# One core, two transformer blocks in float32: the recurrent mixer's steps laid out anew

## The chip, the cores and the metric

One core of a Trainium2 chip runs the whole kernel in one launch. The metric is device time in microseconds (us): 3861.58 us before the change, the median of three runs (3859.82 to 3863.74).

## What is computed

The reference runs two blocks one after the other on 512 tokens of width 1024, all in float32. The change touches one part of the second block, its recurrent mixer, which takes the normalised activations `h` and returns a term that is added to the residual:

```
proj = h @ w_in                       # 1024 -> 2 x 1024: gate, rec
rec  = causal_depthwise_conv(rec)     # 4 taps over the tokens, + bias
r, i = sigmoid(blockwise(rec, w_a) + b_a), sigmoid(blockwise(rec, w_x) + b_x)   # 8 blocks of 128x128
log_a = -8 * r * softplus(-lam);  a = exp(log_a)
bx = sqrt(-expm1(2 * log_a)) * (i * rec)
h_t = a_t * h_(t-1) + bx_t            # scan over the tokens
out = (gelu(gate) * h) @ w_out
```

## The kernel before

Activations lie transposed, features on 128 partitions and the 512 tokens along the free axis, so a width of 1024 is eight chunks ("heads" below, m = 0 to 7). Every float32 product is made of three matmuls on pieces of reduced precision: weights and activations are each split into a high and a low half, and high x high, high x low and low x high are added up in PSUM. A product of one 128-column block of weights with all eight chunks is 24 matmuls (`fm`, lines 317 to 321), one with the output weights by chunk (`wout_k`, lines 767 to 769) 12.

**Weights.** The class `Stream` (from line 51) takes all weight blocks of the kernel in one planned order. A block is fetched by the sync queue into one of three slots (line 102), ScalarE writes its high half `wh` (line 132), VectorE its low half `wl` (line 135), each into one of four buffers. `get` hands out the next block, and before that issues the halves of the blocks up to two places ahead. The engines work through their queues in the order in which the program issues instructions; there is no scheduler that reorders them.

**The mixer** is `rec`, lines 782 to 899. It has sixteen steps u. Steps 0 to 7 make the eight chunks of the recurrent branch, steps 8 to 15 those of the gate branch; each is one product `q` of 24 matmuls. In a step, in the order of issue:
- In steps 2 to 9 `gates_mm(u - 2)` takes two blocks of weights, `ra` and `rx`, and multiplies the halves of chunk u - 2 with both (6 matmuls).
- The chunk that the step before convolved is split into halves (`split`, lines 302 and 303).
- The step's own product is taken up. In steps 0 to 7 VectorE scales it by the row norm `rB` (`conv_start`, line 811), ScalarE makes the last tap and the bias (line 812), GpSimd the first tap (line 818), VectorE the two others (line 820), and GpSimd adds the first one in (line 822). In steps 8 to 14 VectorE scales it into `G` (`evac_g`, line 839).
- `gates(u - 2)`: two sigmoids on ScalarE (lines 803, 805), one product on GpSimd (line 806).
- `decays`: exp and tanh on ScalarE (lines 826, 827) for two heads at a time, in steps 4, 6, 8 and 9; ahead of them `advance` issues the halves of further weights.
- `newton`: one Newton step on the reciprocal that stands behind `a`: a copy on ScalarE (line 832), two operations on VectorE (833, 834), two on GpSimd (835, 836).
- In step 11 the eight square roots (line 884); `scan` for heads 0 to 3 in steps 12 to 14: Gelu on ScalarE (842), a product on GpSimd (843), three operations on VectorE, one of them the scan over the tokens (844 to 846).

After the loop the eight results are split into `hl` (new tiles), with the scans of heads 4 to 7 between them. Then `wout_k` multiplies chunk by chunk, two chunks to a block of weights, and `wout_end` makes the last four output chunks. A block's halves are issued two places ahead, so those of the third output block are issued by `wout_k` for chunk 0, behind everything of the loop.

The row norm `rB` comes from `stat1` (eight small matmuls, line 348; a power on GpSimd, line 354; VectorE, line 360) and `stat2` (a broadcast on TensorE, line 366, copied by ScalarE, line 367), both called after step 0's product.

PSUM has eight banks: two pairs `D`, one pair `E` and two single banks `M`. `dbl` gives pairs of D and E in turn; products and gate pairs of the mixer each take a pair.

Of the kernel before, what the change touches and what calls it, by code (L numbers as in the profile page):

```python
# [15 lines left out]
ALU = mybir.AluOpType  # L16
# [30 lines left out]
def colblock(w, c0, n=P):  # L47
    return w[:, c0:c0 + n].rearrange("(k p) n -> p k n", p=P)

# [132 lines left out]
class Kernel:  # L182
# [553 lines left out]
    def plan_rec(self):  # L736
# [4 lines left out]
        def blk(m):  # L741
            ws.add(("ra", m), wa[m].unsqueeze(1))
            ws.add(("rx", m), wx[m].unsqueeze(1))
# [38 lines left out]
    def rec(self, d, on_x):  # L782
# [10 lines left out]
        taps = {}  # L793

        def gates_mm(m):
            w = (self.ws.get(("ra", m)), self.ws.get(("rx", m), 1))
            q = self.dbl()
            for i in range(2):
                self.fm([(q[:, i], sl)], w[i], xhl[m % 3], nk=1)
            return q  # L800

        def gates(m, q):
# [3 lines left out]
            nc.gpsimd.tensor_tensor(X[:, m], X[:, m], g, ALU.mult)  # L806

        def conv_start(m, q):
            taps[m] = c = self.tmp(TT, tag="ca", bufs=3)[:, :T + 3]
            nc.gpsimd.memset(c[:, 0:3], 0.0)  # L810
            nc.vector.tensor_tensor(c[:, 3:], q, d.rB, ALU.mult)
            nc.scalar.activation(X[:, m], c[:, 3:], AF.Identity, bias=self.v("rec_conv_b_2", m),
                                 scale=self.v("rec_conv_w_2", 24 + m))

        def conv_end(m):
            c, x = taps.pop(m), X[:, m]
            t = self.tmp(T, tag="sq")
            nc.gpsimd.tensor_scalar(t, c[:, 0:T], self.v("rec_conv_w_2", m), 1.0, ALU.mult, ALU.mult)
            for j in (1, 2):
                nc.vector.scalar_tensor_tensor(x, c[:, j:j + T], self.v("rec_conv_w_2", 8 * j + m), x, ALU.mult,  # L820
                                               ALU.add)
            nc.gpsimd.tensor_tensor(x, x, t, ALU.add)
# [6 lines left out]
        def newton(m):  # L829

            z, a, e, f = R[:, m], A[:, m], self.tmp(T, tag="ta"), self.tmp(T, tag="sq")
            nc.scalar.activation(f, a, AF.Copy, scale=0.5, bias=0.5)
            nc.vector.scalar_tensor_tensor(e, z, 1.0, a, ALU.add, ALU.mult)
            nc.vector.scalar_tensor_tensor(e, e, 1.0, z, ALU.subtract, ALU.add)
            nc.gpsimd.tensor_tensor(e, e, f, ALU.mult)
            nc.gpsimd.tensor_tensor(a, a, e, ALU.subtract)
# [3 lines left out]

        def scan(m):
            nc.scalar.activation(G[:, m], G[:, m], AF.Gelu_apprx_tanh)
            nc.gpsimd.tensor_tensor(X[:, m], X[:, m], R[:, m], ALU.mult)
# [4 lines left out]
        ahead = {4: range(2), 6: range(2, 4), 8:range(4,6), 9: range(6, 8)}  # L848
        after = {4: (0,), 5: (1,), 6: (2,),7:(3,),8:(4,),9:(5,), 10: (6, 7)}
        scans = {12: (0,1), 13: (2,), 14: (3,)}  # L850


        for u in range(2 * NK):
            m = u % NK
            w = self.ws.get(("rr" if u < NK else "rg", m))
            q = self.dbl()[:, 0]
            self.fm([(q, sl)], w, d.x)
            if u == 0:
                self.stat1(d)
                self.stat2(d)  # L860
            g = gates_mm(u - 2) if 2 <= u < NK + 2 else None
            if 1 <= u < NK + 1:
                h, l = xhl[(u - 1) % 3]
                self.split(h[:, 0], l[:, 0], X[:, u - 1])
            if u < NK:
                conv_start(m, q)
                conv_end(m)
            else:
                for i in scans.get(u, ()):
                    scan(i)  # L870
                if m < NK - 1:
                    evac_g(m, q)
            if g is not None:
                gates(u - 2, g)

            if u in ahead:
                self.ws.advance(self.ws.i, 0)
            for i in ahead.get(u, ()):
                decays(i)
            for i in after.get(u, ()):  # L880
                newton(i)
            if u == NK + 3:
                for i in range(NK):
                    nc.scalar.activation(R[:, i], R[:, i], AF.Sqrt)
# [1869 lines left out]
```

## Time and profile before

| | |
|---|---|
| device time, median of three runs | 3861.58 us |
| device time of the profiled execution | 3859.96 us |
| its span, first to last instruction | 3858.2 us |
| TensorE, matmuls busy | 3656.6 us (95% of the span) |
| VectorE busy | 2621.0 us (68%) |
| ScalarE busy | 1577.4 us (41%) |
| GpSimd busy | 720.7 us (19%) |

Times in the trace count from the first instruction. PE is TensorE, DVE is VectorE, ACT is ScalarE, POOL is GpSimd. A busy share says how much of the time an engine had an instruction in work; matmuls overlap, so their durations add up to more than the time between their starts. What stands in square brackets at the end of an instruction's row is how long its engine idled before it, and whose instruction ended that.

### The profile page before, as it was taken

Reading aid. Unit: us, or ns where it says so; the run is one execution under the profiler, and the core shown is the slowest. Engines: PE = TensorE matmul, PEld = TensorE weight load, DVE = VectorE, ACT = ScalarE, POOL = GpSimd, SP = SyncE. Lnnn points to the kernel's source line nnn. Section 1 sums busy time; section 2 is a strip of 40 time slices with the busy share of each in tenths; the row PEclk is TensorE's granted clock in tenths of the full one; section 3 lists DMA queues with packets and bytes.
Section 4 is the critical chain, followed back from the end, with each engine's and each line's share of the span. In section 5 each row is a group of like instructions: output and inputs, shape, how many; then the busy total and the mean of one; then the engine's idle time right before and its main releaser. Section 6 shows DMA issues by size and latency. Waiting matters only on the chain. (4 is left out here: it accounts for less than half of the span.)

```text
span 3858.2 us, 54617 instructions
## 1 busy us (share of the span) xinstructions
PE 3656.6 (95%) x21148; PEld 3150.7 (82%) x21148; DVE 2621.0 (68%) x4287; ACT 1577.4 (41%) x2606; POOL 720.7 (19%) x755
## 2 busy tenths in 40 slices
PE   7898999999999978999999998999999999889999
PEld 5887978888887777877789886788977998678898
DVE  7887877765646286544477777677765777766776
ACT  2354523222225275422344447444443444464443
POOL 6334231000012074100100016100020000460000
PEclk8999999999999999999999999999999999899999
DMA  5300043433422442233333322333334333213332
GB/s 176 107 1 23 1 148 95 125 112 118 137 68 88 139 134 77 82 90 90 90 98 102 96 78 81 97 87 96 95 114 124 98 99 99 83 42 102 98 103 75
DMA packets 570400, 363.48 MB, mean 94 GB/s; under 512 B 17719, under 2 KB 546605, under 8 KB 570141
## 3 DMA queue, kind: packets, MB, share of 16 engines
q1 hardware_dynamic: 564317, 346.21, 30.7%
q0 software_dynamic: 3520, 9.59, 0.8%
q8 instruction: 167, 2.74, 0.3%
q10 hardware_dynamic: 2304, 4.20, 0.3%
q14 instruction: 92, 0.75, 0.1%
HBM read 345.72 MB, written 14.20 MB: 93 GB/s over the span
## 5 line engine op out<-in xcount | busy, mean ns | idle before, releaser
L135 DVE TENSOR_TENSOR wl<-ws,wh 128x1024 fp32r<-128x1024 f32 (+3 forms) x474 | 583.3, 1240 | 313.6 <-ACT wh L132 311.2
L132 ACT ACTIVATE wh<-ws 128x1024 fp32r<-128x1024 f32 (+3 forms) x474 | 457.6, 978 | 588.5 <-DVE ws L454 257.3
L562 PE MATMUL D<-ah,wl 128*128 128x256 f32 x1344 | 380.2, 283 | 11.1 <-DVE wl L135 11.1
L560 PE MATMUL D<-ah,wh 128*128 128x256 f32 x1344 | 377.1, 281 | 1.6 <-DVE gu L602 1.6
L561 PE MATMUL D<-al,wh 128*128 128x256 f32 x1344 | 376.4, 280 | 0.9 <-DVE al L495 0.9
L539 PE MATMUL M<-hz,wh 128*128 128x512 f32 x704 | 279.9, 398 | 2.2 <-DVE xT L545 2.2
L540 PE MATMUL M<-hz,wh 128*128 128x512 f32 x704 | 280.4, 398 | 1.0 <-DVE hz L638 0.9
L541 PE MATMUL M<-hz,wl 128*128 128x512 f32 x704 | 278.8, 396 | 0.0
L562 PEld LDWEIGHTS D<-ah,wl 128*128 128x128 f32 x1344 | 252.8, 188 | 18.5 <-DVE wl L135 18.5
L341 POOL TENSOR_TENSOR acc<-acc,t 128x512 f32<-128x512 f32 x36 | 46.9, 1303 | 1171.4 <-ACT t L340 1171.4
L560 PEld LDWEIGHTS D<-ah,wh 128*128 128x128 f32 x1344 | 252.9, 188 | 6.0 <-ACT wh L132 1.9
L561 PEld LDWEIGHTS D<-al,wh 128*128 128x128 f32 x1344 | 252.8, 188 | 5.0 <-DVE al L495 1.3
L321 PE MATMUL D<-ah,wl 128*128 128x512 f32 (+1 forms) x616 | 242.8, 394 | 7.0 <-DVE wl L135 7.0
L317 PE MATMUL D<-ah,wh 128*128 128x512 f32 (+1 forms) x616 | 244.7, 397 | 3.0 <-ACT wh L132 2.7
L319 PE MATMUL D<-al,wh 128*128 128x512 f32 (+1 forms) x616 | 242.8, 394 | 0.8 <-POOL al L2676 0.6
L303 POOL TENSOR_TENSOR hl<-t,hh 128x768 fp32r<-128x768 f32 (+1 forms) x44 | 70.0, 1590 | 797.9 <-ACT hh L302 737.1
L1349 DVE SCALAR_TENSOR_TENSOR as<-ws,S,as 128x256 f32<-128x256 f32 x448 | 202.7, 504 | 3.5
L560 PE MATMUL E<-ah,wh 128*128 128x256 f32 x672 | 188.9, 281 | 6.8 <-ACT t L590 4.0
L562 PE MATMUL E<-ah,wl 128*128 128x256 f32 x672 | 189.9, 283 | 4.7 <-DVE wl L135 4.7
L561 PE MATMUL E<-al,wh 128*128 128x256 f32 x672 | 188.1, 280 | 0.0
L317 PE MATMUL D<-x7h,wh 128*128 128x512 f32 (+1 forms) x464 | 183.8, 399 | 3.0 <-ACT x7h L2671 1.6
L321 PE MATMUL D<-x7h,wl 128*128 128x512 f32 (+1 forms) x464 | 181.4, 394 | 1.1 <-DVE wl L135 1.1
(711 smaller groups left out, 9696.6 us busy)
## 6 DMA issues: line engine op xcount, KB each, us to landing
ws<-in_ffn_w_up_dram SPq DMA_DIRECT2D x104, 512.0 KB
ws<-in_ada_w_dram SPq DMA_DIRECT2D x88, 512.0 KB
t<-in_ffn_w_down_dram SPq DMA_DIRECT2D x128, 256.0 KB
ws<-in_ffn_w_gate_dram SPq DMA_DIRECT2D x88, 256.0 KB
ws<-in_ffn_w_up_dram SPq DMA_DIRECT2D x88, 256.0 KB
wz<-in_ffn_w_gate_dram SPq DMA_DIRECT2D x56, 256.0 KB
wz<-in_ffn_w_up_dram SPq DMA_DIRECT2D x56, 256.0 KB
ws<-in_ffn_w_down_dram SPq DMA_DIRECT2D x32, 384.0 KB
```

What stands on the lines that cost most here:

```text
L132: self.nc.scalar.activation(h[:, :n], t[:, :n], AF.Copy)
L135: self.nc.vector.tensor_tensor(l[:, :n], t[:, :n], h[:, :n], ALU.subtract)
L317: nc.tensor.matmul(o, wh[:, kw + k], xh[:, k0 + k, s], start=a, stop=False)
L319: nc.tensor.matmul(o, wh[:, kw + k], xl[:, k0 + k, s], start=False, stop=False)
L321: nc.tensor.matmul(o, wl[:, kw + k], xh[:, k0 + k, s], start=False, stop=z)
L539: nc.tensor.matmul(q, wh[:, k], h[:, 0, i], start=a, stop=False)
L540: nc.tensor.matmul(q, wh[:, k], h[:, 1, i], start=False, stop=False)
L541: nc.tensor.matmul(q, wl[:, k], h[:, 0, i], start=False, stop=z)
L560: nc.tensor.matmul(o, wh[:, u, k], xh(k0 + k, s), start=start and k == 0, stop=False, skip_group_check=True)
L561: nc.tensor.matmul(o, wh[:, u, k], xl(k0 + k, s), start=False, stop=False, skip_group_check=True)
L562: nc.tensor.matmul(o, wl[:, u, k], xh(k0 + k, s), start=False, stop=stop and k == 3, skip_group_check=True)
L1349: nc.vector.scalar_tensor_tensor(t, w[:, kk], c, t, ALU.mult, ALU.add)
```

## The change

A step takes up the product of the step before it (`qs`) and the gate products of the step before (`gs`). Products go to four single PSUM banks (`psum(M=4)`), gate pairs to `D`. The two gate blocks of a head are one request of 256 columns, `rab`. The broadcast of the row norm (`stat2`) is issued in the middle of step 1's product. `conv` is one function: three taps on VectorE, and the split at its end. GpSimd keeps three-column clears and the power; the products of `gates` and `scan` are on VectorE. `newton` is two operations on VectorE between two copies on ScalarE. `decays` is called for three heads after steps 5 and 8 and for two in step 10, with no `advance` ahead of it; square roots come in two groups of four, in steps 10 and 13. Scans start in step 11, one to a step. The halves of the first three results go to the tiles of the convolved chunks (`Chunks` joins them with new tiles for the other five), from step 13 on.

```diff
--- before.py
+++ after.py
@@ -46,6 +46,16 @@
 
 def colblock(w, c0, n=P):
     return w[:, c0:c0 + n].rearrange("(k p) n -> p k n", p=P)
+
+
+class Chunks:
+
+
+    def __init__(self, aps):
+        self.aps = aps
+
+    def __getitem__(self, i):
+        return self.aps[i[1]] if len(i) == 2 else self.aps[i[1]][:, i[2]]
 
 
 class Stream:
@@ -739,8 +749,7 @@
         wa, wx = I["rec_w_a_2"][0], I["rec_w_x_2"][0]
 
         def blk(m):
-            ws.add(("ra", m), wa[m].unsqueeze(1))
-            ws.add(("rx", m), wx[m].unsqueeze(1))
+            ws.add(("rab", m), [wa[m].unsqueeze(1), wx[m].unsqueeze(1)])
         for m in range(2 * NK):
             ws.add(("rr", m) if m < NK else ("rg", m - NK), colblock(w, (D + m * P) % (2 * D)))
             if 2 <= m < NK + 2:
@@ -790,36 +799,30 @@
         p5 = self.p512
         G = p5.tile([P, NK, T], F32, tag="ah", bufs=2, name="G")
         A = p5.tile([P, NK, T], F32, tag="al", bufs=2, name="A")
-        taps = {}
-
         def gates_mm(m):
-            w = (self.ws.get(("ra", m)), self.ws.get(("rx", m), 1))
-            q = self.dbl()
+            wh, wl = self.ws.get(("rab", m))
+            q = self.bank("D")
             for i in range(2):
-                self.fm([(q[:, i], sl)], w[i], xhl[m % 3], nk=1)
+                self.fm([(q[:, i], sl)], (wh, wl), xhl[m % 3], nk=1, kw=i)
             return q
 
         def gates(m, q):
             nc.scalar.activation(R[:, m], q[:, 0], AF.Sigmoid, bias=self.v("rec_b_a_2", m))
             g = self.tmp(T, tag="tb")
             nc.scalar.activation(g, q[:, 1], AF.Sigmoid, bias=self.v("rec_b_x_2", m))
-            nc.gpsimd.tensor_tensor(X[:, m], X[:, m], g, ALU.mult)
-
-        def conv_start(m, q):
-            taps[m] = c = self.tmp(TT, tag="ca", bufs=3)[:, :T + 3]
+            nc.vector.tensor_tensor(X[:, m], X[:, m], g, ALU.mult)
+
+        def conv(m, q):
+            c, x = self.tmp(TT, tag="ca", bufs=3)[:, :T + 3], X[:, m]
             nc.gpsimd.memset(c[:, 0:3], 0.0)
             nc.vector.tensor_tensor(c[:, 3:], q, d.rB, ALU.mult)
-            nc.scalar.activation(X[:, m], c[:, 3:], AF.Identity, bias=self.v("rec_conv_b_2", m),
+            nc.scalar.activation(x, c[:, 3:], AF.Identity, bias=self.v("rec_conv_b_2", m),
                                  scale=self.v("rec_conv_w_2", 24 + m))
-
-        def conv_end(m):
-            c, x = taps.pop(m), X[:, m]
-            t = self.tmp(T, tag="sq")
-            nc.gpsimd.tensor_scalar(t, c[:, 0:T], self.v("rec_conv_w_2", m), 1.0, ALU.mult, ALU.mult)
-            for j in (1, 2):
+            for j in range(3):
                 nc.vector.scalar_tensor_tensor(x, c[:, j:j + T], self.v("rec_conv_w_2", 8 * j + m), x, ALU.mult,
                                                ALU.add)
-            nc.gpsimd.tensor_tensor(x, x, t, ALU.add)
+            h, l = xhl[m % 3]
+            self.split(h[:, 0], l[:, 0], x)
 
         def decays(m):
             z = R[:, m]
@@ -828,67 +831,76 @@
 
         def newton(m):
 
-            z, a, e, f = R[:, m], A[:, m], self.tmp(T, tag="ta"), self.tmp(T, tag="sq")
-            nc.scalar.activation(f, a, AF.Copy, scale=0.5, bias=0.5)
-            nc.vector.scalar_tensor_tensor(e, z, 1.0, a, ALU.add, ALU.mult)
-            nc.vector.scalar_tensor_tensor(e, e, 1.0, z, ALU.subtract, ALU.add)
-            nc.gpsimd.tensor_tensor(e, e, f, ALU.mult)
-            nc.gpsimd.tensor_tensor(a, a, e, ALU.subtract)
+            z, a, t = R[:, m], A[:, m], self.tmp(T, tag="ta")
+            nc.scalar.activation(a, a, AF.Copy, scale=0.5, bias=0.5)
+            nc.vector.scalar_tensor_tensor(t, z, 1.0, a, ALU.add, ALU.mult)
+            nc.vector.scalar_tensor_tensor(t, t, 2.0, a, ALU.subtract, ALU.mult)
+            nc.scalar.activation(a, t, AF.Copy, scale=-2.0, bias=-1.0)
 
         def evac_g(m, q):
             nc.vector.tensor_tensor(G[:, m], q, d.rB, ALU.mult)
 
+        def roots(*ms):
+            for m in ms:
+                nc.scalar.activation(R[:, m], R[:, m], AF.Sqrt)
+
         def scan(m):
             nc.scalar.activation(G[:, m], G[:, m], AF.Gelu_apprx_tanh)
-            nc.gpsimd.tensor_tensor(X[:, m], X[:, m], R[:, m], ALU.mult)
+            nc.vector.tensor_tensor(X[:, m], X[:, m], R[:, m], ALU.mult)
             nc.vector.scalar_tensor_tensor(X[:, m], A[:, m], 1.0, X[:, m], ALU.add, ALU.mult)
             nc.vector.tensor_tensor_scan(R[:, m], A[:, m], X[:, m], 0.0, ALU.mult, ALU.add)
             nc.vector.tensor_tensor(X[:, m], R[:, m], G[:, m], ALU.mult)
 
-        ahead = {4: range(2), 6: range(2, 4), 8:range(4,6), 9: range(6, 8)}
-        after = {4: (0,), 5: (1,), 6: (2,),7:(3,),8:(4,),9:(5,), 10: (6, 7)}
-        scans = {12: (0,1), 13: (2,), 14: (3,)}
-
-
+        def out(m):
+            self.split(hl[0][:, m], hl[1][:, m], X[:, m])
+
+        hl = tuple(Chunks([xhl[k][i][:, 0] for k in range(3)]) for i in range(2))
+        decs = {5: (0, 1, 2), 8: (3, 4, 5), 10: (6, 7)}
+        newt = {6: (0,), 7: (1,), 8: (2,), 9: (3,), 10: (4,), 11: (5, 6), 12: (7,)}
+        qs, gs = {}, {}
+
+
+
+        self.psum(M=4)
         for u in range(2 * NK):
             m = u % NK
             w = self.ws.get(("rr" if u < NK else "rg", m))
-            q = self.dbl()[:, 0]
-            self.fm([(q, sl)], w, d.x)
+            q = qs[u] = self.mps()
+            if u == 1:
+                self.fm([(q, sl)], w, d.x, NK // 2, last=False)
+                self.stat2(d)
+                self.fm([(q, sl)], w, d.x, NK // 2, NK // 2, NK // 2, first=False)
+            else:
+                self.fm([(q, sl)], w, d.x)
             if u == 0:
                 self.stat1(d)
-                self.stat2(d)
-            g = gates_mm(u - 2) if 2 <= u < NK + 2 else None
+            if 2 <= u < NK + 2:
+                gs[u - 2] = gates_mm(u - 2)
             if 1 <= u < NK + 1:
-                h, l = xhl[(u - 1) % 3]
-                self.split(h[:, 0], l[:, 0], X[:, u - 1])
-            if u < NK:
-                conv_start(m, q)
-                conv_end(m)
-            else:
-                for i in scans.get(u, ()):
-                    scan(i)
-                if m < NK - 1:
-                    evac_g(m, q)
-            if g is not None:
-                gates(u - 2, g)
-
-            if u in ahead:
-                self.ws.advance(self.ws.i, 0)
-            for i in ahead.get(u, ()):
+                conv(u - 1, qs.pop(u - 1))
+            elif u > NK:
+                evac_g(m - 1, qs.pop(u - 1))
+            if 3 <= u < NK + 3:
+                gates(u - 3, gs.pop(u - 3))
+            for i in newt.get(u, ()):
+                newton(i)
+
+            for i in decs.get(u, ()):
                 decays(i)
-            for i in after.get(u, ()):
-                newton(i)
-            if u == NK + 3:
-                for i in range(NK):
-                    nc.scalar.activation(R[:, i], R[:, i], AF.Sqrt)
-        hl = self.acts512()
-        for m in range(NK):
-            self.split(hl[0][:, m], hl[1][:, m], X[:, m])
-            if m == 0:
-                evac_g(NK - 1, q)
-            if m < 4:
-                scan(m + 4)
+            if u in (10, 13):
+                roots(*range(4 * (u == 13), 4 + 4 * (u == 13)))
+            if u >= 11:
+                scan(u - 11)
+            if u >= 13:
+                out(u - 13)
+        z = self.acts512()
+        for i in range(2):
+            hl[i].aps.extend(z[i][:, k] for k in range(3, NK))
+        evac_g(NK - 1, qs.pop(2 * NK - 1))
+        for m in range(3, NK):
+            if m < 6:
+                scan(m + 2)
+            out(m)
 
         def evac(n, q):
             nc.vector.tensor_tensor(self.xT[:, n], q, self.xT[:, n], ALU.add)
@@ -896,6 +908,7 @@
         for k in range(NK):
             self.wout_k("ro", hl, k)
         self.wout_end("ro", hl, evac)
+        self.psum()
         es.close()
 
 
```

## Rows read from the trace of the kernel before

**Rows 1.** Stretches: us; PE, PEld, DVE, ACT, POOL busy (count); clock, DMA share, GB/s.

```profile
2290.50:2475.10 184.60, 162.40 (x635) 124.69 (x634) 133.29 (x148) 99.60 (x147) 79.67 (x64) 0.94 0.26 77
...
2410.00:2420.00 10.00, 6.63 (x16) 4.85 (x17) 9.72 (x11) 0.00 (x0) 3.06 (x2) 0.66 0.20 59
...
2440.00:2450.00 10.00, 9.78 (x35) 7.84 (x36) 3.67 (x4) 1.19 (x2) 0.00 (x0) 0.83 0.75 210
```

**Rows 2.** Waits, 2280 to 2490 us: who waited for whom, us, times, longest.

```profile
DVE wl L135 <- ACT wh L132: 18.8, 18, 2.6
...
DVE t L811 <- PE D L321: 0.4, 1, 0.4
```

**Rows 3.** TensorE in order of time: start us, us, instruction.

```profile
2290.51 0.39 PE L317 MATMUL D<-ah,wh 128*128 128x512 f32 x1
...
2295.90 0.39 PE L321 MATMUL D<-ah,wl 128*128 128x512 f32 x1
...
2299.15 1.12 PE L366 MATMUL M<-t,ones 128*128 128x512 f32 x2 [2.08 <-DVE t L360]
...
2440.22 0.65 PE L769 MATMUL D<-ah,wl 128*128 128x512 f32 x1 [1.19 <-DVE wl L135]
...
2475.14 0.39 PE L317 MATMUL D<-ah,wh 128*128 128x512 f32 x1
```

**Rows 4.** ScalarE in order of time.

```profile
2353.07 0.82 ACT L812 ACTIVATE X<-t,VC 128x512 f32<-128x512 f32 x1 [4.93 <-DVE t L811]
...
2353.79 0.67 ACT L803 ACTIVATE R<-E,VC 128x512 f32<-128x512 f32 x1
...
2354.93 0.30 ACT L132 ACTIVATE wh<-ws 128x128 fp32r<-128x128 f32 x1
...
2355.25 1.28 ACT L826 ACT_TABLE_LOAD   x1
...
2356.55 0.72 ACT L826 ACTIVATE A<-R,rcst 128x512 f32<-128x512 f32 x1
...
2357.93 0.70 ACT L826 ACTIVATE A<-R,rcst 128x512 f32<-128x512 f32 x1
...
2392.85 4.28 ACT L884 ACTIVATE R<-R 128x512 f32<-128x512 f32 x8
...
2443.99 1.06 ACT L132 ACTIVATE wh<-ws 128x1024 fp32r<-128x1024 f32 x1 [3.85 <-DMA ws<-in_rec_w_out_dram]
```

**Rows 5.** VectorE in order of time.

```profile
2352.36 0.68 DVE L811 TENSOR_TENSOR t<-D,rB 128x512 f32<-128x512 f32 x1
...
2354.00 1.54 DVE L820 SCALAR_TENSOR_TENSOR X<-t,VC,X 128x512 f32<-128x512 f32 x2 [0.96 <-POOL t L818]
...
2355.46 0.28 DVE L135 TENSOR_TENSOR wl<-ws,wh 128x128 fp32r<-128x128 f32 x1
...
2426.76 0.68 DVE L303 TENSOR_TENSOR al<-X,ah 128x512 fp32r<-128x512 f32 x1
...
2427.37 0.69 DVE L844 SCALAR_TENSOR_TENSOR X<-A,X 128x512 f32<-128x512 f32 x1
...
2430.03 0.69 DVE L303 TENSOR_TENSOR al<-X,ah 128x512 fp32r<-128x512 f32 x1
...
2438.95 3.49 DVE L135 TENSOR_TENSOR wl<-ws,wh 128x1024 fp32r<-128x1024 f32 x3
...
2445.08 1.23 DVE L135 TENSOR_TENSOR wl<-ws,wh 128x1024 fp32r<-128x1024 f32 x1 [2.64 <-ACT wh L132]
```

**Rows 6.** VectorE's groups by shape, 2290 to 2476 us: busy us, mean ns, idle before.

```profile
L135 DVE TENSOR_TENSOR wl<-ws,wh 128x1024 fp32r<-128x1024 f32 x25 | 37.6, 1515 | 13.3 <-ACT wh L132 13.2
...
L135 DVE TENSOR_TENSOR wl<-ws,wh 128x128 fp32r<-128x128 f32 x16 | 12.3, 767 | 2.4 <-ACT wh L132 2.4
...
L834 DVE SCALAR_TENSOR_TENSOR t<-t,R 128x512 f32<-128x512 f32 x8 | 8.5, 1059 | 0.3
...
L844 DVE SCALAR_TENSOR_TENSOR X<-A,X 128x512 f32<-128x512 f32 x8 | 7.7, 956 | 1.2 <-POOL X L843 1.2
```

## The prediction

> **What bounds the kernel now.** TensorE is busy in 95% of the span (the profile's table), and no line holds a large share of the chain that ended last, so the whole kernel is one long matmul stream and a change is worth what it adds to or takes from TensorE's gaps in its own stage. I therefore read, in this order: the stretches, for the stage; the waits in it; then each engine's instructions in order of time.
>
> The recurrent mixer runs from 2290.51 to 2475.14, where the next SwiGLU's first matmul starts [rows 3]: 184.6 us, in which the clock's mean was 0.94 and VectorE was busy for 133.3 us [rows 1]. Twenty-three steps of a 24-matmul product took 5.39 us, 0.2345 us each, so a product costs 5.63 and a pair of gate blocks (6 matmuls) 1.41 [rows 3]. Sixteen products, eight pairs and the output product (192 matmuls, 45.0) make 146.3, with the statistics 148. The other 36 us are gaps, and slow matmuls behind gaps: the clock is at 0.66 and 0.83 of full speed (a mix of its two levels, 2.4 and 1.2 GHz) in the stretches behind idle time, which costs 3.4 and 1.7 us of ten [rows 1]. The gaps are seldom the fault of a missing product: VectorE waits only 0.4 us for one [rows 2]. It is weights that come late: VectorE's low halves wait 18.8 us for ScalarE's high halves [rows 2], and TensorE waits behind them, as at 2440.22 [rows 3]. ScalarE and VectorE work through in-order queues, so weights wait behind whatever was issued before them.
>
> **The stage ends by one chain.** The output product's fifth chunk needs the third weight block, whose halves are issued behind the last head's halves. Its low half released TensorE at 2440.22 [rows 3]; 48 + 96 matmuls from there (33.8) and 1.7 of slow clock give 2475.7, which is the end seen. So I ask when that low half stands after the change.
>
> **The change, queue by queue.** After it, no tensor operation is left on GpSimd; ScalarE and VectorE pass a head to and fro. I price a step from rows and take 0.05 us for a hand-over between them (rows show 0.03, product scaled to ScalarE, and 0.11 back [rows 4, 5]).
>
> *Convolution step.* The next product's weights: high half 1.06 [rows 4] and the shorter hand-over, 1.09. VectorE's low half is 1.23 alone, three in 3.49, so the next instruction starts after 1.13 [rows 5]. Then the joint gate low half: 256 columns, not in the trace. Its ends are 0.20 (128 columns: 0.28 alone, less the 0.08 by which such starts overlap) and 0.61 (from a 512 low half to the next start [rows 5]); I take 0.33, nearer the smaller size. Then scaling 0.68, ScalarE's tap 0.82, three taps on VectorE (two take 1.54, so 2.31), ScalarE's high half 0.52 (eight activations of this size in 4.28) [rows 4, 5]. With hand-overs: 1.09 + 1.13 + 0.33 + 0.73 + 0.87 + 2.36 + 0.52 = **7.03 us**. TensorE needs 5.63 + 1.41 = 7.04. So this bare chain already fills TensorE's step, and every addition to it comes on top.
>
> *Additions.* Two sigmoids 1.14 [rows 4]. A table load 1.28 each time ScalarE goes from exp/tanh to sigmoid or back; by the code's order there are ten loads before and after. Exp and tanh of a head 1.38 [rows 4], three heads and load 5.4. Newton step: gate product on VectorE 0.61, two operations 1.41, closing ScalarE copy 0.52, hand-overs: 2.74.
>
> *Start.* The statistics' wait of 2.08 [rows 3] goes, since half a product (2.8) now covers it, and about 1.7 of slow clock with it. But the first scaling still needs that broadcast: product to 2296.1, statistics 0.9 (to where the 2.08 begin), half a product 2.8, broadcast 0.6 (two passes, 1.12 at the slow clock [rows 3]), copy 0.6, then scaling, tap, taps and high half 0.7 + 0.9 + 2.4 + 0.5: ScalarE turns to step 2's weights at 2305.8. TensorE is four us earlier, the chain is not.
>
> *Steps 2 to 12*, from 2305.8: 7.03; step 3 +1.14 +1.28 = 9.46; step 4 8.18; step 5 8.18 + 5.4 = 13.57; step 6 8.18 + 1.28 + 2.74 = 12.20; step 7 10.92; step 8 10.92 + 5.4 = 16.31; step 9 (no convolution: two weight blocks 1.9, load, sigmoids, Newton) 7.07; step 10 (weights 0.95, sigmoids 1.15, Newton's two copies 1.04 and 2.26 between them, two loads 2.56, two heads' exp and tanh 2.74, four square roots 2.08) 12.78. That is 2403.3. Step 11 (weights 2.22, scaling 0.60, two Newton steps 1.98 and 2.65, load and Gelu 1.80) 9.25. In steps 5, 8 and 10 the next low half stands behind ScalarE's block of exponentials: VectorE idles there 5.7, 7.1 and 9.1 us, 21.9 in all. The kernel before issues the next weights ahead of its smaller blocks; that call is gone.
>
> *Heads.* From 2412.55, VectorE sets the pace. A scan cycle with its low half takes 3.27 [rows 5]; the multiplication that came from GpSimd adds 0.72 (0.69 and a hand-over). Step 12 (weights 1.09 and 1.13, scaling 0.60, Newton's two operations 1.34, scan 3.38) 7.54; steps 13 to 15 (weights, Gelu branch's scaling, scan, low half) 5.71 each: 2437.2. Then the last scaling 0.60, three heads at 3.98, two low halves 1.29: 2451.05, and the third block's low half at 2452.2. That the first three heads' halves go to spare tiles, and so need not wait for the last product, helps nothing: VectorE's scans are late next.
>
> *End.* 2452.2 + 33.8 + 2.3 of slow clock (between the 1.7 and 3.4 of rows 1) = 2488.3 against 2475.14: **+13.1 us**.
>
> *Edits at nothing.* The gate blocks' sixteen transfers stay on the sync queue, paired in eight slots, with more lead, since three requests are now one and a half steps. ScalarE's one long wait for data, 3.85 us, is at the output weights [rows 4]; a pair that came late in the loop would cost about as much once, and the slower chain is the cover. GpSimd keeps the three-column clears and the power, with an empty queue. Four PSUM banks for products replace one pair and two: a bank is free three steps before its reuse. Opening this pool may make the first product wait for the last read of the old banks. No row shows it; the ends are 0 and the nearest gap of that kind, 2.08 [rows 3] and 1.7 of slow clock after it; I take 0, since the code reads the banks that are written first well before.
>
> **Contention, the rule that speaks for the change.** Sixteen low halves of 128 columns took 0.77 us in the mean, 0.28 alone; 25 of 1024 took 1.52 instead of 1.23; a Newton operation 1.06 and the scan's first 0.96 instead of 0.69 [rows 5, 6]: 7.8 + 7.1 + 3.0 + 2.1 = 20.0 us lost while GpSimd worked. My sum has this relief in it, for every duration above is one taken with GpSimd idle. The Trainium skill, "SBUF — State Buffer", section "Who interferes with whom", says that a VectorE instruction with two SBUF inputs contends with a GpSimd one that reads SBUF, and that one blocks the other whole. The trace agrees in direction; by that rule alone the change would be a gain, 3852 by the first rival's sum where mine gives 3873.
>
> **Rivals.**
> 1. *VectorE's work, not its waits, sets the end* (faster). Relief 20.0 us, and 1.1 from joining halves (16 at 0.28 against 8 at 0.42, an estimate between the rows' sizes); against it 8 third taps (0.77), 8 gate products (0.61), 8 root products (0.72): 16.8. Net -4.3, and the start's 3.8: 3860 - 8 = 3852, a little less with the relief of smaller groups. It decides if VectorE's idle time in the stage stays under the 51 us of now (184.6 - 133.3); by my sum it is about 69 (197.7 - 129). For: it is busy for 72% of the stage. Against: an in-order chain does not give back a wait. The rule named above points here.
> 2. *The blocks of exponentials are covered* (no change): if the weights behind them are already split, half or more of the 21.9 us goes, 3873 - 11 = 3862. Against: at each request exactly two more are split, which reaches one product ahead.
> 3. *The pool opening stalls the start*: +3.8, 3877. For: the pool is opened right at the stage's first product. Against: banks, not pools, are waited for elsewhere.
> 4. *The pick-up of last step's products does not do what it says*: it can save no more than the 0.4 us that VectorE waited [rows 2]. That holds within the forecast.
>
> **How the numbers follow.** The profiled execution took 3859.96 us (span 3858.2); the median shown is 3861.58, 1.6 above. 3859.96 + 13.1 = 3873.1. Hand-overs of 0.03 to 0.12 (some 50 on the chain) give -1 to +3.5, the joint half's bounds over six steps -0.8 to +1.7, the clock at most +1.1, the median +1.6: the likeliest case's own range is 3869 to 3882. Chances: forecast with rivals 3 and 4, 0.69; rival 2, 0.14; rival 1, 0.17. A measurement here can tell about 0.2% (7.7 us) from no change; the forecast lies above that. The range goes down to 3856 to take in rival 2.
>
> **What would show it.** Right: the stage ends near 2488; VectorE's low halves wait some 39 us for ScalarE's high halves; TensorE has gaps of 6 to 7 us at products 7 and 10 and before the output product's fifth chunk; low halves of 1024 columns at 1.23; no GpSimd tensor operation. Wrong: a stage under 180 us, or gaps of TensorE that all stay under 3 us; then the queues overlap where I chained them.

## The result and the profile after

The changed kernel took 3885.55 us, the median of four runs (3881.84 to 3892.82), beside 3862.09 for the kernel before (four runs): ratio 1.0063, 95% interval 1.0046 to 1.0081. The sign was right; the time lies 12.5 us above the forecast and 3.5 above the top of the range.

The mixer is measured from the end of the last matmul ahead of it (its start and 0.2345) to the first matmul of the next SwiGLU. Before, that is 2290.51 to 2475.14 [rows 3], 184.63 us. Now it is 2299.70 to 2503.35, **203.65 us**, 19.0 more. The first row below is that stretch, the others are ten microseconds behind TensorE's longest gaps; the columns are those of [rows 1].

```profile
2299.70:2503.35 203.65, 170.86 (x635) 129.40 (x635) 125.67 (x164) 103.76 (x147) 9.72 (x16) 0.88 0.24 69
...
2358.80:2368.80 10.00, 9.10 (x28) 6.54 (x29) 6.04 (x9) 4.78 (x7) 0.00 (x0) 0.77 0.24 66
2399.10:2409.10 10.00, 9.90 (x31) 7.42 (x32) 7.65 (x10) 7.27 (x11) 0.00 (x0) 0.73 0.41 110
2466.40:2476.40 10.00, 9.88 (x29) 7.38 (x30) 4.78 (x5) 2.91 (x3) 0.00 (x0) 0.68 0.67 192
```

VectorE is busy for 125.67 us where it was 133.3 [rows 1], and the stage is longer all the same: its idle time grew from 51 to 78 us. The granted clock's mean fell from 0.94 to 0.88, and behind each gap it is a mix of the two levels, 2.4 and 1.2 GHz, as before.

The waits of the stretch 2290 to 2513 us, in the form of [rows 2]:

```profile
DVE wl L145 <- ACT wh L142: 36.2, 19, 9.4
...
PE M L327 <- ACT wh L142: 18.6, 6, 6.9
```

Weights are late: VectorE waits 36.2 us for ScalarE's high halves (18.8 before), and TensorE's products wait 18.6 us for them. TensorE in order of time, to be held against [rows 3]:

```profile
2301.78 0.52 PE L327 MATMUL M<-ah,wh 128*128 128x512 f32 x1 [1.93 <-DVE xT L555]
...
2358.81 0.80 PE L327 MATMUL M<-ah,wh 128*128 128x512 f32 x1 [4.79 <-ACT wh L142]
...
2399.16 0.79 PE L327 MATMUL M<-ah,wh 128*128 128x512 f32 x1 [6.90 <-ACT wh L142]
...
2466.41 0.79 PE L776 MATMUL D<-ah,wh 128*128 128x512 f32 x1 [5.11 <-ACT wh L142]
...
2503.35 0.40 PE L327 MATMUL D<-ah,wh 128*128 128x512 f32 x1
```

The first row is a gap that the kernel before does not have: the mixer's first product goes to a bank M, and waits until VectorE has read the SwiGLU's last output from there. The next two are products 7 and 10, behind blocks of exponentials, the fourth is the output product's fifth chunk. ScalarE in order of time, first two equal steps, then a block of exponentials:

```profile
2318.42 0.63 ACT L312 ACTIVATE rxh<-X 128x512 fp32r<-128x512 f32 x1 [2.47 <-DVE X L822]
2318.95 1.35 ACT L142 ACTIVATE wh<-ws 128x1024 fp32r<-128x1024 f32 x2
2322.23 0.81 ACT L819 ACTIVATE X<-t,VC 128x512 f32<-128x512 f32 x1 [1.92 <-DVE t L818]
2325.51 0.63 ACT L312 ACTIVATE rxh<-X 128x512 fp32r<-128x512 f32 x1 [2.46 <-DVE X L822]
2326.04 1.35 ACT L142 ACTIVATE wh<-ws 128x1024 fp32r<-128x1024 f32 x2
...
2392.66 1.28 ACT L829 ACT_TABLE_LOAD   x1
...
2398.07 1.99 ACT L142 ACTIVATE wh<-ws 128x1024 fp32r<-128x1024 f32 x2
```

VectorE in order of time, the same places and the end:

```profile
2320.03 1.56 DVE L145 TENSOR_TENSOR wl<-ws,wh 128x1024 fp32r<-128x1024 f32 x2 [0.26 <-ACT wh L142]
2321.51 0.68 DVE L818 TENSOR_TENSOR t<-M,rB 128x512 f32<-128x512 f32 x1
2323.14 2.33 DVE L822 SCALAR_TENSOR_TENSOR X<-t,VC,X 128x512 f32<-128x512 f32 x3 [0.95 <-ACT X L819]
2326.17 0.69 DVE L313 TENSOR_TENSOR rxl<-X,rxh 128x512 fp32r<-128x512 f32 x1 [0.70 <-ACT rxh L312]
...
2399.14 2.36 DVE L145 TENSOR_TENSOR wl<-ws,wh 128x1024 fp32r<-128x1024 f32 x2 [7.21 <-ACT wh L142]
...
2464.66 1.89 DVE L313 TENSOR_TENSOR al<-X,ah 128x512 fp32r<-128x512 f32 x3
2466.47 3.49 DVE L145 TENSOR_TENSOR wl<-ws,wh 128x1024 fp32r<-128x1024 f32 x3
```

From 2318.95 to 2326.04 is one bare convolution step, 7.09 us. The two rows of engines interlock: VectorE waits 0.26, 0.95 and 0.70 for ScalarE, and ScalarE waits 1.92 and 2.46 for VectorE. Neither has anything else that it may do, because what could fill the wait stands behind the waiting instruction in its own queue; above all ScalarE's next weights stand behind `rxh`, which waits for VectorE's three taps. VectorE's groups by shape in the mixer, columns as in [rows 6]:

```profile
L145 DVE TENSOR_TENSOR wl<-ws,wh 128x1024 fp32r<-128x1024 f32 x25 | 31.9, 1285 | 35.1 <-ACT wh L142 34.9
...
L837 DVE SCALAR_TENSOR_TENSOR t<-t,A 128x512 f32<-128x512 f32 x8 | 5.5, 692 | 0.3
L850 DVE SCALAR_TENSOR_TENSOR X<-A,X 128x512 f32<-128x512 f32 x8 | 5.5, 692 | 0.3
...
L145 DVE TENSOR_TENSOR wl<-ws,wh 128x256 fp32r<-128x256 f32 x8 | 3.3, 418 | 0.0
```

The contention is gone as expected: 1.29 us a low half instead of 1.52, 0.69 for the Newton operation instead of 1.06 and for the scan's first instead of 0.96 [rows 6], and eight joint gate halves of 0.42 in place of sixteen of 0.77.

### The profile page after: what moved, and what is told of

Same layout as the page of the kernel before. It is cut to its first block, busy times and chain, and to the rows that moved or that the text cites. A ratio compares the mean times of both kernels' runs of the same rounds, so it can differ in the third digit from the quotient of the medians.

```text
span 3891.0 us, 54553 instructions
## 1 busy us (share of the span) xinstructions
PE 3678.4 (95%) x21148; PEld 3167.8 (81%) x21148; DVE 2613.9 (67%) x4303; ACT 1582.1 (41%) x2606; POOL 650.3 (17%) x707
## 5 line engine op out<-in xcount | busy, mean ns | idle before, releaser
L145 DVE TENSOR_TENSOR wl<-ws,wh 128x1024 fp32r<-128x1024 f32 (+3 forms) x466 | 569.1, 1230 | 335.2 <-ACT wh L142 332.6
L331 PE MATMUL D<-ah,wl 128*128 128x512 f32 (+1 forms) x528 | 207.0, 392 | 3.9 <-DVE wl L145 3.9
L327 PE MATMUL D<-ah,wh 128*128 128x512 f32 (+1 forms) x528 | 208.9, 396 | 0.3 <-ACT ah L2684 0.3
L329 PE MATMUL D<-al,wh 128*128 128x512 f32 (+1 forms) x528 | 207.5, 393 | 0.8 <-POOL al L2689 0.6
```

The lines of the kernel that those rows point to most:

```text
L145: self.nc.vector.tensor_tensor(l[:, :n], t[:, :n], h[:, :n], ALU.subtract)
L327: nc.tensor.matmul(o, wh[:, kw + k], xh[:, k0 + k, s], start=a, stop=False)
L329: nc.tensor.matmul(o, wh[:, kw + k], xl[:, k0 + k, s], start=False, stop=False)
L331: nc.tensor.matmul(o, wl[:, kw + k], xh[:, k0 + k, s], start=False, stop=z)
```

## The experiments

Every kernel below computes everything that the reference does. The mixer comes from one profiled execution of each; two of the changed kernel differ by 1.4 us. Where an expectation names a ledger, it is a sum of both queues' durations and hand-overs, made as the prediction makes it. The median of before is that of its runs on the same chip, side by side with the kernel.

| kernel | median us | before us | ratio, 95% interval | mixer us |
|---|---|---|---|---|
| before | | | | 184.63 |
| changed kernel, first time | 3885.55 | 3862.09 | 1.0046 to 1.0081 | 203.65 |
| changed kernel, again | 3884.48 | 3865.66 | 1.0035 to 1.0065 | 202.29 |
| first product in a D bank | 3883.08 | 3865.66 | 1.0030 to 1.0058 | 200.00 |
| weights ahead of exponentials | 3879.74 | 3865.66 | 1.0027 to 1.0056 | 201.28 |
| other order within a step | 3858.92 | 3865.66 | 0.9972 to 0.9990 | 177.17 |
| before, all on VectorE | 3861.41 | 3862.85 | 0.9985 to 1.0004 | 179.75 |
| before, late pick-up | 3884.99 | 3862.85 | 1.0034 to 1.0066 | 205.34 |
| two products back on GpSimd | 3887.19 | 3862.85 | 1.0042 to 1.0078 | 205.42 |
| scaling first | 3869.53 | 3862.83 | 1.0008 to 1.0028 | 190.85 |
| hand-overs interleaved | 3869.42 | 3862.83 | 1.0009 to 1.0029 | 190.26 |
| third output block early | 3878.93 | 3862.83 | 1.0025 to 1.0057 | 196.06 |
| order, D bank and early block | 3850.03 | 3862.85 | 0.9941 to 0.9973 | 167.97 |

**The changed kernel again**, unaltered, as the yardstick:

> The changed kernel once more, unaltered. In the first profile of it the mixer took 203.6 us (from the end of the SwiGLU's last matmul to the first matmul of the next SwiGLU), 19.0 more than before, and the rest of the kernel 13.8 us more, 9.2 of it ahead of the mixer. Theory: the change acts inside the mixer alone; the mixer takes 203 to 204 us again, and what the rest took was this execution's own, so it differs here by several us. Rival: the changed program also slows the rest (other code, other placement of buffers); then the same 13.8 us, at the same places, stand in this profile.

Against fifteen runs of before on the same chip it is slower by 18.8 us (3884.48 - 3865.66), and its mixer is longer by 17.7 (202.29 - 184.63): all but some 1 us of the loss lies in the mixer. Outside the mixer all these kernels issue the same work, and the thirteen profiled spans less their mixers run from 3672.1 to 3687.3 us; before's was 3673.5, the changed kernel's first 3687.3 and its second 3682.9. The 13.8 us by which the first two spans differ beyond their mixers (3891.0 - 3858.2 - 19.0) are not shown to be work of the change. Ahead of the mixer the first run was 9.2 us later than before and the second 4.8, while the kernel with its hand-overs interleaved, further down, was 2.9 earlier. Behind it both runs lost some 4.5, of which 2.8 at one place; the kernel with the first product in a D bank has none of these 2.8. What makes that part vary stays open.

**Start: the first product in a bank of the gate blocks.**

```
-            q = qs[u] = self.mps()
+            q = qs[u] = self.mps() if u else self.bank("D")[:, 0]
```

> The first product goes to a bank that was not part of the pool opened anew. Theory: the wait for the last read of the old banks (1.93 us) and the slow clock behind it delay the broadcast of the row norm and with it the whole chain of VectorE and ScalarE: the mixer gets shorter by 3.5 to 4.2 us, to 199.5 to 200. Rival: the chain catches up while TensorE has slack in the first steps: less than 1 us.

TensorE in order of time shows the first product without a wait, at full speed:

```profile
2295.41 0.40 PE L551 MATMUL M<-hz,wl 128*128 128x512 f32 x1
2295.65 0.39 PE L327 MATMUL D<-ah,wh 128*128 128x512 f32 x1
```

The mixer is 2.3 to 3.65 us shorter, where I had expected 3.5 to 4.2. ScalarE's weights for step 2 tell it more closely; the changed kernel's own row for them is further up (2318.95):

```profile
2311.20 1.35 ACT L142 ACTIVATE wh<-ws 128x1024 fp32r<-128x1024 f32 x2
```

They start 15.55 us behind the stage's start (2311.20 - 2295.65), against 19.25 and 19.22 in the two runs of the changed kernel: 3.7 less. The rest of the spread is the stage's end, which took 1.3 less in the second run than in the first and in this one. It is the bank that the first product goes to that costs the 3.7.

**Weights ahead of the exponentials**, the call that the change dropped:

```
+            if u in decs:
+                self.ws.advance(self.ws.i, 0)
             for i in decs.get(u, ()):
```

> Ahead of each block of exponentials the next weight halves are issued, as in the kernel before. Rival 2 of the prediction: the 21.9 us that VectorE stands behind these blocks are the loss, so half or more of it goes: mixer shorter by 11 us or more. Theory (in-order exchange between the two engines): the halves come earlier, but the scaling's tap on ScalarE stands behind the block just the same, so VectorE's wait moves from the low half to the tap: shorter by 1 to 3 us only.

Only 1.0 to 2.4 us came back, although 22 us of waits stand behind these blocks. VectorE in order of time shows where it now stands behind the three blocks:

```profile
2352.25 0.43 DVE L145 TENSOR_TENSOR wl<-ws,wh 128x256 fp32r<-128x256 f32 x1 [4.62 <-ACT wh L142]
...
2392.45 1.23 DVE L145 TENSOR_TENSOR wl<-ws,wh 128x1024 fp32r<-128x1024 f32 x1 [5.26 <-ACT wh L142]
...
2412.40 0.69 DVE L836 SCALAR_TENSOR_TENSOR t<-R,A 128x512 f32<-128x512 f32 x1 [6.36 <-ACT A L835]
```

The call moves one weight block ahead each time. The next thing that needs ScalarE (the gate block, the second product's weights, the copy of a Newton step) still stands behind the exponentials, and VectorE waits 4.6, 5.3 and 6.4 us for it instead of 5.8, 7.2 and 9.4. So the wait was moved more than removed. This run does not settle what the blocks themselves cost; that they are not the loss against before is seen from the other order, next, which leaves them in place.

**The order within a step.** The same instructions; VectorE scales the last step's product ahead of the next weights, the sigmoids go ahead of the split, and the gate product and the Newton step's two VectorE operations between a head's high and low half:

```
+            if 2 <= u < NK + 1:
+                scaled(u - 1, qs.pop(u - 1))
+            elif u > NK:
+                evac_g(m - 1, qs.pop(u - 1))
             w = self.ws.get(("rr" if u < NK else "rg", m))
...
+                last_tap(u - 1)
+            g = gates(u - 3, gs.pop(u - 3)) if 3 <= u < NK + 3 else None
...
+                other_taps(u - 1)
+                h, l = xhl[(u - 1) % 3]
+                nc.scalar.activation(h[:, 0], X[:, u - 1], AF.Copy)
+            if g is not None:
+                gated(u - 3, g)
...
+                nc.vector.tensor_tensor(l[:, 0], X[:, u - 1], h[:, 0], ALU.subtract)
```

> Same instructions on the same engines; only their order within a step differs: the scaling stands ahead of the weights' halves, tap, sigmoids and Newton's first copy stand together on ScalarE, then the three taps, the gate product and Newton's two operations together on VectorE, then the split's low half and Newton's closing copy. Theory: VectorE's and ScalarE's waits for each other set the end, not their work: each step sheds about 3 us, the mixer gets shorter by 20 to 26 us (to about 180), the total comes to 3860 to 3866 and the waits of low halves for high halves fall from about 39 to under 30 us. Rival: the work moved to VectorE sets the end: less than 4 us.

The mixer falls by 25.1 to 26.5 us, to 177.17, VectorE's waits for high halves within the stage from 34.9 to 27.5, and the kernel is 0.2% faster than before; its total lies 1.1 under the range that I gave. Behind the three blocks of exponentials VectorE still waits 4.4, 6.0 and 8.8 us, so most of the gain was made elsewhere. VectorE in order of time, one whole step and the scaling of the next but one:

```profile
2327.35 0.69 DVE L821 TENSOR_TENSOR t<-M,rB 128x512 f32<-128x512 f32 x1
2327.95 1.55 DVE L145 TENSOR_TENSOR wl<-ws,wh 128x1024 fp32r<-128x1024 f32 x2
2329.42 2.33 DVE L830 SCALAR_TENSOR_TENSOR X<-t,VC,X 128x512 f32<-128x512 f32 x3
2331.66 0.69 DVE L816 TENSOR_TENSOR X<-X,t 128x512 f32<-128x512 f32 x1
2332.45 0.69 DVE L908 TENSOR_TENSOR rxl<-X,rxh 128x512 fp32r<-128x512 f32 x1
2333.05 0.68 DVE L821 TENSOR_TENSOR t<-M,rB 128x512 f32<-128x512 f32 x1
...
2339.54 0.69 DVE L821 TENSOR_TENSOR t<-M,rB 128x512 f32<-128x512 f32 x1 [0.70 <-PE M L331]
```

The step has one operation more than the bare one (the gate product) and lasts 5.70 us (2327.35 to 2333.05) where that took 7.09: no row of it has a wait. While ScalarE makes its tap, VectorE has low halves to do; while ScalarE makes the high half, VectorE has the gate product. It is shorter than TensorE's 7.04, and at 2339.54 VectorE waits for a product: there TensorE is the bound again.

**Its two parts, each alone in the changed kernel.** First only the scaling ahead of the weights (the first four added lines above), then only the interleaving, with the scaling left behind the weights:

> The changed kernel with one part of the other order alone: VectorE scales the last step's product ahead of the next weights' low halves, as the kernel before did, and everything else stays. Theory (each hand-over that waits behind the weights costs a step its length): the chain of a step gets shorter by about 1.1 to 1.7 us in eleven steps; by the ledger the mixer goes from 202.1 to 190.6, so 189 to 193 us, total 9 to 13 below the changed kernel. Rival (the order of the taps, the gate product and the Newton step is what counts, the scaling only moves the wait): mixer 199 or more.

> The changed kernel with the other part alone: the scaling stays behind the weights; the sigmoids are issued ahead of the split of the head, the gate product and the Newton step's two VectorE operations go between the head's high and low half. Theory: while one engine does its half of a hand-over the other has work, by the ledger the mixer goes from 202.1 to 189.1, so 188 to 192 us, and with the run of the scaling alone the two parts add up to the 25 us of the run with both. Rival (one of the two parts carries nearly all): one of the two runs at 199 or more, the other at 180 or less.

190.85 and 190.26: 11.4 to 12.8 and 12.0 to 13.4 us less than the changed kernel. Their sum, 23.5 to 26.2, comes within 2 us of the 25.1 to 26.5 of both together. The rival, one part with nearly all, falls.

**Before's order, all tensor operations on VectorE.** Six calls `nc.gpsimd` become `nc.vector`, of which:

```
-            nc.gpsimd.tensor_tensor(x, x, t, ALU.add)
+            nc.vector.tensor_tensor(x, x, t, ALU.add)
```

> The kernel before, with its order of steps untouched; only the tensor operations that GpSimd did (a head's first tap and its addition, the gate product, two operations of the Newton step, the scan's root product) are put on VectorE. This is the engine part of the change alone. Theory (the order and the pick-up lose the time, the engine move is about even): what VectorE gains by being free of contention, some 10 us on the chain, is about what the added operations cost it; mixer 182 to 186 us against 184.6 before, total within 0.2% of before. Rival (the move to VectorE is itself the loss, because VectorE's queue becomes the chain): mixer 195 or more, total +10 us or more against before.

```profile
2292.75:2472.50 179.75, 160.44 (x635) 123.58 (x634) 139.46 (x196) 99.48 (x147) 9.70 (x16) 0.94 0.28 79
```

That is the stretch of its mixer; in its groups by shape, gate low halves are at 0.285 us:

```profile
L135 DVE TENSOR_TENSOR wl<-ws,wh 128x128 fp32r<-128x128 f32 x16 | 4.6, 285 | 0.6 <-ACT wh L132 0.6
```

VectorE has 139.46 us of work instead of 133.3 [rows 1], and the mixer is 4.9 us shorter, 2 under the range I gave. The total can't be told from before. The engine move is not the loss.

**Before's engines, the change's pick-up.** All GpSimd operations stay, and a step still takes up its own gate products; four banks M, the statistics in product 1, and the step takes up the last product behind its own weights:

```
             if 1 <= u < NK + 1:
+                conv_start(u - 1, qs.pop(u - 1))
+                conv_end(u - 1)
                 h, l = xhl[(u - 1) % 3]
                 self.split(h[:, 0], l[:, 0], X[:, u - 1])
-            if u < NK:
-                conv_start(m, q)
-                conv_end(m)
...
```

> The kernel before with all its GpSimd operations kept, and only the pick-up changed: four product banks, the product of a step scaled, tapped and split in the next step behind that step's weights, statistics in the middle of product 1. Theory (the late pick-up, which puts the whole convolution, the split and the gates of one step into one chain behind the weights, is the loss): mixer 194 us by a ledger without contention and up to 10 us more with it, 194 to 205, total +9 to +20 us against before. Rival (the pick-up is harmless and the loss comes with VectorE's added work): mixer within 3 us of the 184.6 of before.

```profile
2287.47:2492.81 205.34, 173.90 (x636) 129.26 (x635) 132.22 (x148) 99.56 (x147) 75.98 (x64) 0.88 0.24 69
```

205.34, just past the upper end: this part alone loses 20.7 us, as much as the whole change, of which some 2 to 4 are the start's by the run with a D bank (the first product has the same gap here, 1.92). Before, a chunk was convolved in the step that made it and split one step later, so its chain spread over two steps; now it runs within one, and the wait of a head's low half for its high half grows, first before and then here:

```profile
DVE rxl L303 <- ACT rxh L302: 2.3, 2, 2.0
```

```profile
DVE rxl L303 <- ACT rxh L302: 17.4, 8, 2.4
```

Two reserves belong to this. The chain of this run passes through GpSimd's addition, which the change has not, so its 20.7 us are not the change's own term by term. And a chain within one step need not be long: the other order keeps it there and is shorter than before. What loses is the late pick-up behind the weights, in the order that the change gave it.

**Two products back on GpSimd** in the changed kernel (the gate product and the scan's root product):

```
-            nc.vector.tensor_tensor(X[:, m], X[:, m], g, ALU.mult)
+            nc.gpsimd.tensor_tensor(X[:, m], X[:, m], g, ALU.mult)
...
-            nc.vector.tensor_tensor(X[:, m], X[:, m], R[:, m], ALU.mult)
+            nc.gpsimd.tensor_tensor(X[:, m], X[:, m], R[:, m], ALU.mult)
```

> The changed kernel with two of the moved operations put back on GpSimd: the gate product and the scan's root product; the order stays. Theory (VectorE's queue sets the pace only in the heads, and contention gives part of it back): mixer 198 to 202 us against 202.3 to 203.7 of the changed kernel, total 0 to 5 us below it. Rival (the move to VectorE is what made the change slower): mixer under 192 us.

A miss: 205.42, 1.8 to 3.1 us longer instead of shorter. Two places show the contention that comes back. First VectorE in order of time, then GpSimd:

```profile
2370.24 1.36 DVE L836 SCALAR_TENSOR_TENSOR t<-R,A 128x512 f32<-128x512 f32 x1 [0.98 <-ACT A L835]
...
2431.37 2.20 DVE L851 TENSOR_TENSOR_SCAN R<-A,X 128x512 f32<-128x512 f32 x1
...
2435.14 1.77 DVE L313 TENSOR_TENSOR rxl<-X,rxh 128x512 fp32r<-128x512 f32 x1
2436.84 2.29 DVE L145 TENSOR_TENSOR wl<-ws,wh 128x1024 fp32r<-128x1024 f32 x1
```

```profile
2369.76 1.28 POOL L813 TENSOR_TENSOR X<-X,t 128x512 f32<-128x512 f32 x1 [10.28 <-ACT t L812]
...
2430.63 7.42 POOL L849 TENSOR_TENSOR X<-X,R 128x512 f32<-128x512 f32 x4 [15.04 <-ACT R L845]
```

The 0.6 us that the gate product took of VectorE comes back as 0.67 on the Newton operation beside it (1.36 instead of 0.69; so in four of the eight, and 1.30 in a fifth). The last four root products come in one burst of 7.42 us, and the scan, a split and a low half beside it take 2.20, 1.77 and 2.29 instead of 1.23, 0.69 and 1.23. The Trainium skill, "Perfetto Trace Analysis", section "Optimizing Scalar/DVE Operations", warns that moving operations between GpSimd and VectorE might not help because they share a read port; these rows agree.

**The third output block's halves ahead of the last heads:**

```
         evac_g(NK - 1, qs.pop(2 * NK - 1))
+        self.ws.advance(self.ws.i, 0)
```

> The changed kernel with the third output block's halves issued ahead of the last heads, and nothing else. Theory (the stage's end is set by that block's low half behind the last heads' halves, as the step on the end said): the gap before the output product's fifth chunk goes, the last heads set the end; mixer 195 to 198 us against 202.3 to 203.7, total 4 to 7 below the changed kernel. Rival (the last heads' halves are just as late): mixer 201 or more.

The mixer is 196.06 us, 6.2 to 7.6 less; the total moved less, from 18.8 above before to 16.1 (its remainder outside the mixer was 3682.6 in the profile). The gap of 5.11 is gone: behind the third chunk TensorE waits 1.10, 0.92 and 0.90 us, each time for a head's low half, so the last heads set the end.

**The best version**: other order, first product in a D bank, early block (ahead of the last scaling):

> The changed kernel with three edits together: the other order within a step (as in the run with the order changed, mixer 177.2), the first product in a bank of the gate blocks, and the third output block's halves issued ahead of the last heads. Theory (the parts add up): -2.3 to -4 us from the first bank and -4 to -6 from the early halves, mixer 167 to 171 us, total 13 to 17 us below before on this chip, a ratio of 0.9955 to 0.9965. Rival (the early halves only move the wait to the last heads, and the start is covered by the new order): mixer 175 to 178, total as in the run with the order changed.

```profile
2290.61:2458.58 167.97, 155.95 (x635) 121.86 (x634) 123.63 (x164) 103.28 (x147) 9.70 (x16) 0.96 0.29 84
```

The mixer is 167.97 us, 16.7 shorter than before, and the total 12.8 us below before (3862.85 - 3850.03), a ratio of 0.9957. The parts add up in the mixer: the two small edits take another 9.2 off the 177.17. The total's gain is 0.2 short of the range I gave and 3.9 less than the mixer's; that difference lies in the part outside the mixer and is not explained.

## Why the prediction was right and wrong

The forecast was a mixer of 197.8 us (2488.3 - 2290.51). It was 203.65 and 202.29. The chain can be followed by the starts of ScalarE's weights for steps 2 to 13 in the first profile (the second has the same start and steps within 0.04 us, and 68.75 at the end):

| | forecast us | measured us |
|---|---|---|
| stage's start to step 2's weights | 15.3 | 19.25 (2299.70 to 2318.95) |
| step 2 | 7.03 | 7.09 |
| 3, 4 | 9.46, 8.18 | 9.66, 8.25 |
| 5, 6, 7 | 13.57, 12.20, 10.92 | 13.77, 12.79, 11.03 |
| 8, 9, 10 | 16.31, 7.07, 12.78 | 16.53, 7.25, 13.11 |
| 11, 12 | 9.25, 5.32 | 9.48, 5.38 |
| step 13's weights to the stage's end | 70.4 | 70.06 (2433.29 to 2503.35) |

Step 12's forecast here is the sum of the prediction's terms on ScalarE's side (weights 2.22, scaling 0.60, a Newton step 1.98, closing copy 0.52), and 70.4 is what its total then leaves. One slip is in the start: the terms listed there add up to 2305.5, not to 2305.8, so 15.0 and not 15.3.

- **The step that failed: "Opening this pool may make the first product wait ... I take 0."** The first product waited 2.08 us (2299.70 to 2301.78), and its 24 matmuls then took 7.23 (to 2309.01) instead of 5.63, at a granted clock of 0.76 in the mean. That is 3.7 of the 3.95 that the start is over, and without it the time would have come to 3881.9, just inside the range. My reason, that the banks written first had been read well before, was an error: VectorE's residual addition was still to read the SwiGLU's last output. The gap was rival 3, which priced it at 3.8; the run with a D bank takes 3.7 off the start and 2.3 to 3.65 off the mixer.
- **Hand-overs, mis-sized.** Eleven steps took 114.34 against 112.09, each longer by 0.06 to 0.59, most in step 6. With this 2.25 and the start's 3.95, less 0.35 at the end, the 5.9 of the first mixer are all placed.
- **The base.** The other 6.6 of the 12.5, more than the failed step, lie outside the mixer: the sum was made against one execution whose remainder (3673.5) is near the low end of the thirteen. My range held 1.6 for that, the median against the one execution. Before's own runs on three later occasions spread from 3857.1 to 3873.0. Side by side on one chip the change costs 18.8, where I said 13.1.
- **Right: the chain.** The bare step at 7.03 was 7.09. Idle times of 5.7, 7.1 and 9.1 behind the exponentials were 5.77, 7.21 and 9.35. VectorE's waits for high halves were 36.2 for some 39, TensorE's gap at product 10 was 6.9; those at product 7 and before the fifth output chunk, 4.8 and 5.1, were shorter than the 6 to 7 I gave. The joint gate half, taken at 0.33, delays the next start by 0.35 (1.48 from 2320.03 to 2321.51, less 1.13). No GpSimd tensor operation is left, and low halves that stand alone take 1.23.
- **Rival 1, VectorE's work sets the end, falls** for the change: VectorE does less and idles 78 us. It names a real gain, though: in before's order the same engine move takes 4.9 us off the mixer. In the run with two products put back, VectorE's Newton operation ended 0.56 us after the gate product beside it (2370.24 + 1.36 against 2369.76 + 1.28), little less than its own 0.69: it stood nearly until GpSimd was done. The rule of the Trainium skill, "SBUF — State Buffer", section "Who interferes with whom", that one of the two is held off by the other, agrees with these rows and with the sign of the engine move.
- **Rival 2, the exponentials' blocks are covered, falls** for the change: VectorE's waits behind them stand as forecast, and one weight block put ahead of each brings back 1.0 to 2.4 us. The waits are still there in the best version, 4.4, 6.0 and 8.8 us, and whether more can be had from them was not tried.
- **Where I read too little into my own sum.** I wrote that the bare chain "already fills TensorE's step, and every addition to it comes on top", and left the order of issue at that. Some twelve microseconds hang on the place of one instruction a step, VectorE's scaling, and about as many on what stands between a high and a low half.

## What to carry to other kernels

Where two in-order engines hand one chunk to and fro, lay out each queue so that behind every hand-over there is work that does not need it: the same instructions took 202 or 177 us. Before taking up a product a step later, add up the chain that then has to fit into one step, and compare it with the bound's step. A long wait in the list of waits is the place where a delay comes due, not where it is made; moving the instruction that is waited for tells the two apart, if the trace then shows that nothing else waits at the same place.

## What the runs showed of the hardware

GpSimd's contention is dear where its operations come in a burst: four products in 7.42 us (1.86 each, against 1.28 for a gate product) lengthened three VectorE operations beside them by 0.97, 1.08 and 1.06 us. I had not expected that a single gate product costs VectorE as much by its presence on GpSimd (0.67) as when VectorE runs it itself (0.6). And the work outside the mixer, the same in all kernels, spread over 15 us between executions, which is more than most of the differences in question. The stage's own length, which repeats within 1.4 us, told them apart.
